# Norm factors put in at eviction, twelve pairs begun ahead, and one PSUM pool, in a hybrid block of two Strassen FFNs and a mixer

## The chip, the core and the metric

The kernel runs on one core of one Trainium2 chip. The metric is the device time of one execution in microseconds (us); lower is better. TensorE (PE in the profile) multiplies matrices into PSUM, a memory of eight banks of 128 x 512 f32; VectorE (DVE), ScalarE (ACT) and GpSimd (POOL) work elementwise; SyncE (SP) issues most DMAs, which move tiles between DRAM and the on-chip SBUF. Each engine runs its own instructions in the order in which the compiler wrote them, and semaphores hold an instruction until its inputs are there.

## The reference: what is computed

The input x has 1024 tokens of width 1024. One layer is applied:

```
h = x + 0.5 * swiglu(rmsnorm(x) , w1_in [1024 x 5632], w1_out [2816 x 1024])
h = h + mixer(rmsnorm(h))          # short convolutions and a gated delta rule
h = h + 0.5 * swiglu(rmsnorm(h), w2_in, w2_out)
out = rmsnorm(h)

swiglu(y) = (silu(y @ w_gate) * (y @ w_up)) @ w_out
rmsnorm(x, w) = x * rsqrt(mean(x * x, axis=-1) + 1e-6) * w
```

All of it is f32. Since rmsnorm multiplies each token by one factor, and each channel by one gain, (factor * gain * x) @ W is the same as factor * ((gain * x) @ W): the factor of a token may be put in before or after a product with weights.

## The kernel before

Tokens lie along the free axis, in two halves of 512; channels lie along the 128 partitions, so x is `h[half][d]`, eight tiles of 128 x 512 per half.

**Products.** A number is held as a rounded part (hi) and the rest (lo), and a product of two such numbers is three matmuls of 128 x 128 by 128 x 512 (`mm3`, lines 196 to 200: whi by hi, whi by lo, wlo by hi). Splitting a tile costs a copy on ScalarE (line 104) and a subtraction on VectorE (line 105). `prod` (line 202) is one block product: four k steps, 12 matmuls into one bank.

**Seven products instead of eight.** Each matrix product is cut in two by two blocks and done by a Strassen-Winograd scheme. For the FFN's input side, a pair is one gate tile and one up tile of 128 columns; `Pair` (line 357) holds its seven products. P1 = B11 by A11 and P2 = B21 by A12 need only the first half of tokens; P1 stays in one bank while it is copied out (`copy_p1`, line 385, ScalarE) and P2 is added onto it in the same bank (`run_p2`). These two are the pair's heads (`head1`, `head2`). The other five products, the body (line 416), use S1 to S4 and A22, which are sums of both halves of tokens (`Blocks.sums`, line 325), and weight sums T1 to T4 made on GpSimd (`pool_tt`) or, for the first two pairs, on VectorE. VectorE evicts them (lines 414 to 452). There are 22 pairs.

**Order.** Work is a list of tasks with three stages (`run_tasks`, line 124): the loads of a task are issued up to nine tasks ahead, its preparation (splits, weight sums) up to four ahead, then it runs. The compiler's scheduler then orders each engine's instructions by priority and estimated readiness, except those under `keep_in_program_order`, which stay behind everything traced earlier on their engine. `later` and `tick` put small steps behind a number of `mm3`s.

**The first stage, in order.** Five pairs' heads run before anything that needs the second half of tokens (`EARLY` = 5). `first_heads` (line 687) loads the eight x tiles, the constants and four B11 tiles; keeps TensorE going with idle matmuls on zeros (`idle`, 34 + 6 + 5 of them); squares and adds the x tiles, sums them over partitions on TensorE (lines 247 to 250), makes the factors (`factor`, line 221, a power on GpSimd), spreads them over partitions (`spread`, line 266, four transposes into a bank), scales x (`norm1`, line 305) and splits it (`split1`). Then come the B11 products of four pairs k step by k step, the fifth pair's P1, and the five P2. The factors of the second half come from row sums of squares (`row_square`, `by_rows`); when they are spread, `x.sums(0)` starts to make S1 and S2. `all_pairs` (line 461) then runs pairs 0 and 1 together, with the heads of two more pairs (`INSIDE` = 2) among their products, then pairs 2 and 3, then one pair at a time; from pair 6 on, the heads of pair i + 1 stand between the products of pair i.

The heads' results P1 and C11 wait in SBUF, in a ring of 21 temporaries, until the body of their pair uses them. The same `all_pairs` serves the mixer's q, k, v projection (six pairs) and the second FFN.

**PSUM.** Each of the three large stages (first FFN with the projection, mixer, second FFN) opens its own PSUM pool (`scoped`, line 660): one tag `ps` with eight banks, or, in the mixer, `mm` and `aux` with four each.

Of the kernel before, what the change touches and what calls it, by code (L numbers as in the profile page):

```python
# [12 lines left out]
P = 128  # L13
# [45 lines left out]
def tile_hybrid(  # L59
# [82 lines left out]
    def psum(tag="ps"):  # L142
        bufs = {"ps": 8, "mm": 4, "aux": 4}[tag]
        return scope["ps"].tile([P, 512], F32, name=f"ps_{tag}", tag=tag, bufs=bufs)
# [64 lines left out]
    class Norm:  # L209
# [25 lines left out]
        def as_they_land(self, idle):  # L235

            idle(34)
            for d in range(KT):
                sq = slot(F32, "sq")
                tc.keep_in_program_order(nc.scalar.activation(out=sq, in_=self.hh[d], func=AF.Square))  # L240
                if d:
                    nc.vector.tensor_tensor(out=self.acc, in0=self.acc, in1=sq, op=ALU.add)
                else:
                    self.acc = sq
# [5 lines left out]
            idle(6)  # L250
# [106 lines left out]
    class Pair:  # L357
# [5 lines left out]
        def __init__(self, x, srcs, first, done):  # L363
            self.x, self.srcs, self.first, self.done = x, srcs, first, done
            self.r, self.t, self.w, self.pinned, self.tt = {}, {}, {}, False, pool_tt
# [14 lines left out]
        def run_p1(self):  # L380
            self.x_ps = psum()
            prod(self.x_ps, self.w.pop("B11"), self.x.b["A11"], True)
            self.copy_p1()

        def copy_p1(self):
            self.p1 = temp4(F32, "p1")
            ins = nc.scalar.copy(out=self.p1[:, 3:HALF + 3], in_=self.x_ps)  # L387
            if self.pinned:
                tc.keep_in_program_order(ins)

        def run_p2(self):
            prod(self.x_ps, self.w.pop("B21"), self.x.b["A12"], False)
            self.done("C11", self.first(self.x_ps))
# [67 lines left out]
    def all_pairs(pairs, x, norm2, between={}, twos=(0, 2)):  # L461


        inside = pairs[EARLY:EARLY + INSIDE]

        def heads_of(some):
            for p in some:
                task(*p.head1())
                task(*p.head2())
# [35 lines left out]
    def gate_pair(x, w_in, j, gs, store):  # L505
        t = {}

        def first(ps):
            c = temp4(F32, "c11")
# [1142 lines left out]
```

## Time and profile before

| | us |
|---|---|
| median of three runs | 1825.29 |
| lowest and highest | 1824.38, 1825.42 |
| the profiled execution's own time | 1825.61 |
| its span, first to last instruction | 1823.9 |
| TensorE busy | 1790.0 (98%) |
| VectorE busy | 1315.3 (72%) |
| ScalarE busy | 742.9 (41%) |
| GpSimd busy | 678.0 (37%) |
| first real product starts (line 197) | 17.80 |

The page gives the busy time of each engine, the span in slices, DMA queues, the chain of work that ended last, and the costliest groups of instructions. Views of the trace give the same by group, by stretch of time, or in order of time; a row in order of time has the start, the duration, the engine, the line, the operation, what it writes and reads, and in brackets how long the engine had been idle and what released it. Matmuls overlap: one of 128 x 512 lasts about 0.39 us but the next starts 0.23 us after it, so the distance of starts is the price of one.

### The profile page before, as it was taken

To read this page: it belongs to the slowest core of one execution; us is meant where nothing else is said; L and a number is where in the kernel's file an instruction comes from. 1 tells how busy PE (TensorE), PEld (TensorE's weight loads), DVE (VectorE), ACT (ScalarE), POOL (GpSimd) and SP (SyncE) were. 2 spreads that over 40 slices of the span, in tenths; PEclk is the share of its full clock that TensorE was granted. 3 is DMA by queue.
4 is the path that set the end of the run, shared out by engine and by line. 5 is a ranking of instruction groups with operands and counts; after the bars stand their busy time and mean duration, and the time that the engine had idled before them with its cause. 6 is when DMAs were issued, how large, how long until landed. Compare 5 with 4: busy or idle time off the path is not lost.

```text
span 1823.9 us, 24890 instructions
## 1 busy us (share of the span) xinstructions
PE 1790.0 (98%) x8509; PEld 1462.3 (80%) x8509; DVE 1315.3 (72%) x2040; ACT 742.9 (41%) x1482; POOL 678.0 (37%) x478
## 2 busy tenths in 40 slices
PE   9999999999999999999899999999999999999997
PEld 6788888888888887777778887788888888888885
DVE  8966666667775888978867576887656666677675
ACT  7423222233534554478242343552222222344443
POOL 0365544445341412325321113006544544435252
PEclk9999999999999999999999999999999999999998
DMA  7243443436984543478664485523433443488642
GB/s 261 70 167 122 136 147 125 135 116 217 326 265 139 168 150 112 137 245 262 221 198 142 133 286 182 177 75 117 160 133 116 144 139 132 163 279 285 215 145 87
DMA packets 194320, 311.41 MB, mean 171 GB/s; under 512 B 28176, under 2 KB 48656, under 8 KB 194192
## 3 DMA queue, kind: packets, MB, share of 16 engines
q1 hardware_dynamic: 191168, 304.51, 50.4%
q10 hardware_dynamic: 3024, 5.30, 0.8%
q8 instruction: 67, 1.10, 0.2%
q14 instruction: 61, 0.50, 0.1%
HBM read 226.87 MB, written 82.86 MB: 170 GB/s over the span
## 4 chain that ended last, share of the span: by engine, by line
PE 85%; DVE 6%; DMA 3%; ACT 3%; issue 2%; POOL 1%; SPq 0%; ACTq 0%; POOLq 0%; DVEq 0%
PE ps_ps L197 24%; PE ps_ps L199 24%; PE ps_ps L198 24%; PE ps_mm L197 3%; PE ps_mm L199 2%; PE ps_mm L198 2%; PE ps_aux L982 1%; DVE cv L884 1%; DMA raw<-w_in 1%; DVE wlo L105 1%; DVE xb L1142 1%; DVE sv L1138 1%; DMA h<-xT 1%; PE ps_aux L1008 0%; DMA qkv_dr<-cv 0%
## 5 line engine op out<-in xcount | busy, mean ns | idle before, releaser
L197 PE MATMUL ps_ps<-hi,whi 128*128 128x512 f32 x1400 | 546.0, 391 | 3.8 <-DVE h L1478 1.5
L198 PE MATMUL ps_ps<-lo,whi 128*128 128x512 f32 x1400 | 545.1, 389 | 0.1
L199 PE MATMUL ps_ps<-hi,wlo 128*128 128x512 f32 x1400 | 544.7, 390 | 0.1
L105 DVE TENSOR_TENSOR wlo<-T,whi 128x512 fp32r<-128x512 f32 x244 | 226.5, 941 | 131.8 <-ACT whi L104 131.1
L105 DVE TENSOR_TENSOR wlo<-raw,whi 128x512 fp32r<-128x512 f32 x280 | 252.9, 914 | 92.1 <-ACT whi L104 87.6
L112 POOL TENSOR_TENSOR T<-raw 128x512 f32<-128x512 f32 x132 | 205.0, 1553 | 302.8 <-DVE wlo L105 108.8
L197 PEld LDWEIGHTS ps_ps<-hi,whi 128*128 128x128 f32 x1400 | 262.7, 188 | 63.7 <-ACT p L387 2.6
L199 PEld LDWEIGHTS ps_ps<-hi,wlo 128*128 128x128 f32 x1400 | 262.8, 188 | 56.1 <-DVE wlo L105 1.7
L198 PEld LDWEIGHTS ps_ps<-lo,whi 128*128 128x128 f32 x1400 | 262.9, 188 | 54.8 <-DVE lo L105 0.8
L197 PE MATMUL ps_ps<-ghi,whi 128*128 128x512 f32 x616 | 241.3, 392 | 0.0
L199 PE MATMUL ps_ps<-ghi,wlo 128*128 128x512 f32 x616 | 240.9, 391 | 0.4 <-DVE wlo L105 0.4
L198 PE MATMUL ps_ps<-glo,whi 128*128 128x512 f32 x616 | 240.6, 391 | 0.0
L104 ACT CAST whi<-raw 128x512 fp32r<-128x512 f32 x280 | 169.0, 617 | 64.0 <-DMA raw<-w_out 21.0
L104 ACT CAST whi<-T 128x512 fp32r<-128x512 f32 x244 | 146.2, 616 | 73.8 <-POOL T L112 34.2
L197 PE MATMUL ps_mm<-hi,whi 128*128 128x512 f32 x384 | 158.5, 413 | 1.2 <-DVE u L452 1.2
L105 DVE TENSOR_TENSOR glo<-raw,ghi 128x512 fp32r<-128x512 f32 x154 | 126.9, 824 | 43.2 <-ACT ghi L104 42.6
L199 PE MATMUL ps_mm<-hi,wlo 128*128 128x512 f32 x384 | 151.6, 395 | 0.0
L198 PE MATMUL ps_mm<-lo,whi 128*128 128x512 f32 x384 | 151.0, 393 | 0.0
L199 PEld LDWEIGHTS ps_ps<-ghi,wlo 128*128 128x128 f32 x616 | 115.8, 188 | 26.5 <-DVE wlo L105 1.0
L198 PEld LDWEIGHTS ps_ps<-glo,whi 128*128 128x128 f32 x616 | 116.1, 188 | 25.6
L197 PEld LDWEIGHTS ps_ps<-ghi,whi 128*128 128x128 f32 x616 | 115.7, 188 | 25.2
L387 ACT COPY p<-ps_ps 128x512 f32<-128x512 f32 x50 | 29.0, 585 | 241.1 <-PE ps_ps L199 241.0
(239 smaller groups left out, 2263.5 us busy)
## 6 DMA issues: line engine op xcount, KB each, us to landing
raw<-w_in SPq DMA_DIRECT2D x264, 256.0 KB, 4.6
raw<-w_out SPq DMA_DIRECT2D x154, 256.0 KB, 4.2
raw<-w_qkv SPq DMA_DIRECT2D x36, 256.0 KB, 3.1
f1S<-S SPq DMA_DIRECT2D x33, 256.0 KB, 5.1
raw<-f1A SPq DMA_DIRECT2D x33, 256.0 KB, 3.6
raw<-f1S SPq DMA_DIRECT2D x33, 256.0 KB, 3.6
f2S<-S SPq DMA_DIRECT2D x33, 256.0 KB, 4.8
raw<-f2A SPq DMA_DIRECT2D x33, 256.0 KB, 4.0
```

What stands on the lines that cost most here:

```text
L104: tc.keep_in_program_order(nc.scalar.copy(out=hi, in_=src))
L105: nc.vector.tensor_tensor(out=lo, in0=src, in1=hi.bitcast(F32), op=ALU.subtract)
L112: tc.keep_in_program_order(nc.gpsimd.tensor_tensor(out=out, in0=in0, in1=in1, op=op))
L197: nc.tensor.matmul(out=ps, lhsT=whi, rhs=xhi, start=start, stop=False, skip_group_check=True)
L198: nc.tensor.matmul(out=ps, lhsT=whi, rhs=xlo, start=False, stop=False, skip_group_check=True)
L199: nc.tensor.matmul(out=ps, lhsT=wlo, rhs=xhi, start=False, stop=stop, skip_group_check=True)
L387: ins = nc.scalar.copy(out=self.p1[:, 3:HALF + 3], in_=self.x_ps)
L884: nc.vector.scalar_tensor_tensor(out=acc, in0=u[:, i:i + HALF], scalar=vcol(wc + i), in1=acc, op0=ALU.mult, op1=ALU.add)
L982: nc.tensor.matmul(out=ps[:, sl], lhsT=lhs[:, sl], rhs=rhs[:, sl], start=start, stop=stop)
L1138: nc.vector.tensor_tensor(out=tv, in0=lrow[:, lo:hi].unsqueeze(2).broadcast_to([nb, n, j + 1]), in1=xrow[:, 0:j + 1].unsqueeze(1).broadcas ...
L1142: nc.vector.tensor_tensor(out=xv, in0=xv, in1=tv, op=ALU.subtract)
```

## The change

- In the first FFN, x is multiplied by its gain alone and split as it lands (`split_raw`); the factor of a first-half token is multiplied in when P1 is copied out and before Silu of C11, both on VectorE, from a copy of the spread factors in SBUF (`rb0`, which shares its place with the later `rb2`). x is still scaled in place afterwards, for S1 to S4. Loads are issued in the order x tile 0, four B11, x tiles 1 to 7, constants; rows for the second half's sums and the second half itself follow at given tasks.
- The idle matmuls are 12 instead of 45. The sums of squares, the factors and their spread come behind the four B11 products; the fifth pair's P1 stands between sums and spread.
- Nine pairs' heads run ahead (before five) and three among pairs 0 and 1 (before two). Of these twelve, pairs 5 to 11 write P1 and C11 to DRAM (`spill`, `put`) and read them back while the pair before runs (`fetch`).
- In all three uses of `all_pairs`, the P1 of an inside pair stands ahead of the last k step of the S1 and S2 products, or between two other products, instead of right before its P2.
- One PSUM pool serves the whole kernel, with tags `mm` and `aux` of four banks; a request for `ps` takes them in turn.

```diff
+    pp = ctx.enter_context(tc.tile_pool(name="pp", bufs=1, space=PS))
+    turn = [0]
+
+    def psum(name="ps"):
+        tag = name
+        if name == "ps":
+            tag = ("mm", "aux")[turn[0] % 2]
+            turn[0] += 1
+        return pp.tile([P, 512], F32, name=f"ps_{name}", tag=tag, bufs=4)
...
+        def spill(self, p1, c11):
+            self.dr = p1, c11
+
+        def put(self, i, tile_):
+            if self.dr is not None:
+                nc.sync.dma_start(out=self.dr[i], in_=tile_[:, 3:HALF + 3])
+
+        def fetch(self):
+            self.p1 = temp4(F32, "p1")
+            nc.sync.dma_start(out=self.p1[:, 3:HALF + 3], in_=self.dr[0])
+            c = temp4(F32, "c11")
+            nc.sync.dma_start(out=c[:, 3:HALF + 3], in_=self.dr[1])
+            self.done("C11", c)
+
         def copy_p1(self):
             self.p1 = temp4(F32, "p1")
-            ins = nc.scalar.copy(out=self.p1[:, 3:HALF + 3], in_=self.x_ps)
-            if self.pinned:
-                tc.keep_in_program_order(ins)
+            if self.rb is None:
+                nc.scalar.copy(out=self.p1[:, 3:HALF + 3], in_=self.x_ps)
+            else:
+                nc.vector.tensor_tensor(out=self.p1[:, 3:HALF + 3], in0=self.x_ps, in1=self.rb, op=ALU.mult)
+            self.put(0, self.p1)
...
+        now, soon = inside[:max(1, len(inside) - 1)], inside[max(1, len(inside) - 1):]
...
                 for k in range(KH):
+                    if k == KH - 1:
+                        task(*now[0].head1())
                     task(lambda k=k: [p.both(k) for p in pairs[:2]])
-                heads_of(inside[:1])
+                for p in now[1:]:
+                    task(*p.head1())
+                for p in now:
+                    task(*p.head2())
...
-                    for t in two:
-                        task(*t)
-                if a == 0 and n == 2:
-                    heads_of(inside[1:])
+                    task(*two[0])
+                    for p in soon if a == 0 and n == 2 else ():
+                        task(*p.head1())
+                    task(*two[1])
+                    for p in soon if a == 0 and n == 2 else ():
+                        task(*p.head2())
...
         for i in range(twos[-1] + 2, len(pairs)):
             body = list(pairs[i].body())
-            if EARLY + INSIDE <= i + 1 < len(pairs):
+            if i + 1 < len(pairs) and pairs[i + 1].dr is not None:
+                body[2:2] = [(None, pairs[i + 1].fetch)]
+            if n_early + n_inside <= i + 1 < len(pairs):
                 body[2:2] = [pairs[i + 1].head1()]
                 body[4:4] = [pairs[i + 1].head2()]
...
         def first(ps):
             c = temp4(F32, "c11")
+            if rb is not None:
+                nc.vector.tensor_tensor(out=c[:, 3:HALF + 3], in0=ps, in1=rb, op=ALU.mult)
+                ps = c[:, 3:HALF + 3]
             nc.scalar.activation(out=c[:, 3:HALF + 3], in_=ps, func=AF.Silu)
...
+        def split_raw(d):
+            src, gain = h[0][d], x.gain(d)
+            hi, lo = slot(F32R, "hi"), slot(F32R, "lo")
+            tc.keep_in_program_order(nc.scalar.activation(out=hi, in_=src, func=AF.Copy, scale=gain))
+            nc.vector.scalar_tensor_tensor(out=lo, in0=src, scalar=gain, in1=hi.bitcast(F32),
+                                           op0=ALU.mult, op1=ALU.subtract)
+            x.b["A11" if d < KH else "A12"][d % KH] = hi, lo
...
             for k in range(KH):
-                first(k)
...
+                task(lambda k=k: run(k))
+            task(norms[0].all_landed)
+            f, g, l = early[4].head1()
+            task(lambda: f(False), g, l)
+            task(scaled)
+            task(*early[5].head1())
+            for i in range(4):
+                second(i)
+            for i in range(4, len(early)):
+                if i == 5:
+                    task(norms[1].spread)
+                if i + 2 < len(early):
+                    task(*early[i + 2].head1())
+                second(i)
-        g_dr = ffn_in(x, norms, w1_in, "f1", first_heads)
+        g_dr = ffn_in(x, norms, w1_in, "f1", first_heads, rb0, 5, 9, 3)
```

`second(i)` is the P2 of early pair i with steps of the second half beside it: row squares, `by_rows`, `norm1`, `begin2`, and the loads of rows and of the second half. `scaled` spreads the first half's factors, copies them to `rb0` and scales the P1 of the first five pairs out of PSUM.

More of the change, by code (lines that the diff above doesn't have):

```diff
@@ L233, in reduce, with landed, all_landed @@
             self.factor(cp[:, 0:4])
[L235 to L244, printed above, removed]
+        def landed(self, d):
+            sq = slot(F32, "sq")
+            tc.keep_in_program_order(nc.scalar.activation(out=sq, in_=self.hh[d], func=AF.Square))
+            if d:
+                nc.vector.tensor_tensor(out=self.acc, in0=self.acc, in1=sq, op=ALU.add)
+            else:
+                self.acc = sq
+        def all_landed(self):
             cp = psum(self.bank)
@@ L459, in body, with all_pairs @@
             yield run_p3, lambda: self.ready("B22")
[L461 to L469, printed above, removed]
+    def all_pairs(pairs, x, norm2, between={}, twos=(0, 2), n_early=EARLY, n_inside=INSIDE):
+        inside = pairs[n_early:n_early + n_inside]
+        now, soon = inside[:max(1, len(inside) - 1)], inside[max(1, len(inside) - 1):]
         for p in pairs[:2]:
@@ L523, in done, with ffn_in @@
                 store(j, hf)
-        return Pair(x, (w_in[j, 0], w_in[j, 1]), first, done)
+        pair = Pair(x, (w_in[j, 0], w_in[j, 1]), first, done)
+        pair.rb = rb
+        return pair
     G_BLOCKS = ("A11", "A12", "A22", "S1", "nS2", "S3", "S4")
-    def ffn_in(x, norms, w_in, name, start=None):
+    def ffn_in(x, norms, w_in, name, start=None, rb=None, kept=EARLY + INSIDE, early=EARLY, inside=INSIDE):
         gs = {}
@@ L554, in store @@
                     later(8 + 5 * i, lambda args=args: make(*args))
-        pairs = [gate_pair(x, w_in, j, gs, store) for j in range(NJ)]
-        if start is None:
-            early_heads(pairs[:EARLY])
-        else:
-            start(pairs)
-        all_pairs(pairs, x, norms[1])
+        pairs = [gate_pair(x, w_in, j, gs, store, rb) for j in range(NJ)]
+        for i in range(kept, early + inside):
+            pairs[i].spill(dram.tile([P, HALF], F32, name=f"{name}p{i}"), dram.tile([P, HALF], F32, name=f"{name}c{i}"))
+        (start or early_heads)(pairs[:early])
+        all_pairs(pairs, x, norms[1], n_early=early, n_inside=inside)
         return g_dr
@@ L703, in first_heads, with get_rows @@
             idle_ps = psum()
[L705 to L712 removed]
+            for _ in range(12):
+                tc.keep_in_program_order(
+                    nc.tensor.matmul(out=idle_ps, lhsT=zero[:, 0:P], rhs=zero, start=True, stop=True))
             for p in four:
                 p.x_ps = psum()
[L715 to L720 removed]
+            for d in range(KT):
+                split_raw(d)
+                if d == 0:
+                    for p in four:
+                        p.ready("B11")
+                if d == KH - 1:
+                    for e in range(KT):
+                        norms[0].landed(e)
+                elif d < KH:
+                    pass
+            rows2 = []
+            def get_rows(*bs):
+                for b in bs:
+                    for i in range(2):
+                        rows2.append(slot(F32, "xtok"))
+                        tc.keep_in_program_order(nc.sync.dma_start(out=rows2[-1], in_=xtok[b][:, i, :]))
             def run(k):
@@ L725, in run @@
                     mm3(p.x_ps, w[0][:, ks], w[1][:, ks], *x.b["A11"][k], k == 0, k == KH - 1)
-                if k == KH - 1:
-                    for p in four:
-                        p.w.pop("B11")
-                        p.copy_p1()
-                    norms[1].spread()
-            for k in range(KH):
-                first(k)
-            def then():
-                for d in range(KH, KT):
-                    first(d)
-                norms[1].by_rows()
-                for k in range(KH):
-                    x.begin2(k)
@@ L742, in first_heads, with scaled @@
-            task(lambda: run(0), then, lambda: get_x(1, 0, 4, 1, 5, 2, 6, 3, 7))
-            for k in range(1, KH):
-                task(lambda k=k: run(k))
-            task(*early[4].head1())
-            for p in early:
-                task(*p.head2())
-        g_dr = ffn_in(x, norms, w1_in, "f1", first_heads)
+            def scaled():
+                norms[0].spread()
+                nc.scalar.copy(out=rb0, in_=norms[0].rb)
+                for p in four:
+                    p.w.pop("B11")
+                    p.copy_p1()
+                early[4].copy_p1()
```

67 lines of the change are left out of this document (33 added, 34 removed).

## The prediction

> **What bounds the kernel now.** I read the head of the page first, then the busy time by stage, then the first 31 us of TensorE in order of time, then TensorE's waits one by one.
>
> ```profile
> span 1823.9 us, 24890 instructions
> PE 1790.0 (98%) x8509; PEld 1462.3 (80%) x8509; DVE 1315.3 (72%) x2040; ACT 742.9 (41%) x1482; POOL 678.0 (37%) x478
> PE 85%; DVE 6%; DMA 3%; ACT 3%; issue 2%; POOL 1%; SPq 0%; ACTq 0%; POOLq 0%; DVEq 0%
> ```
>
> TensorE is busy 98% of the span and carries 85% of the chain that ended last. So what counts is when its first real product starts, what stands between its products, and nothing else until another engine falls behind it.
>
> ```profile
> core 0: us, PE busy (x) PEld busy (x) DVE busy (x) ACT busy (x) POOL busy (x), PEclk, DMA share, GB/s
> 0.00:17.80 17.80, 13.80 (x58) 6.06 (x58) 9.23 (x18) 9.62 (x17) 3.09 (x9) 1.00 0.92 329
> 29.20:46.60 17.40, 17.31 (x79) 14.07 (x77) 17.40 (x30) 14.17 (x27) 0.00 (x0) 1.00 0.37 121
> 46.60:60.00 13.40, 13.40 (x60) 10.87 (x59) 13.40 (x23) 5.75 (x10) 0.00 (x0) 1.00 0.13 42
> 111.00:139.00 28.00, 28.00 (x123) 22.47 (x121) 17.16 (x24) 4.94 (x9) 13.48 (x10) 1.00 0.49 168
> 177.00:405.00 228.00, 228.00 (x1007) 188.79 (x1006) 146.30 (x168) 65.70 (x120) 111.09 (x72) 1.00 0.39 132
> ```
>
> Two prices come from here. In steady state 1007 matmuls take 228 us, 0.2264 us each, so a product of 12 matmuls is 2.72 us. And from 29.2 to 60 us VectorE is never idle: 53 instructions in 30.8 us, 0.58 us each (0.60 below). It is the second bound of the first stage and must be watched.
>
> ```profile
> 1.32 9.70 PE L708 MATMUL ps_ps<-zero 128*128 128x512 bf16 x34 [1.32 <-DVE zero L702]
> 5.13 0.15 PEld L708 LDWEIGHTS <-zero 128*128 128x128 bf16 x1 [0.28 <-issue]
> 5.56 0.15 PEld L708 LDWEIGHTS <-zero 128*128 128x128 bf16 x1 [0.28 <-issue]
> 5.89 4.63 PEld L708 LDWEIGHTS <-zero 128*128 128x128 bf16 x22 [0.18 <-issue]
> 12.87 1.05 PE L248 MATMUL ps_ps<-one,sq 128*128 128x1 f32 x8 [1.85 <-DVE sq L242]
> 13.79 1.46 PE L708 MATMUL ps_ps<-zero 128*128 128x512 bf16 x6
> 14.21 1.40 POOL L225 TENSOR_TENSOR rs<-ms,cs 128x4 f32<-128x4 f32 x1 [11.92 <-DVE ms L223]
> 15.66 0.65 PE L271 MATMUL ps_ps<-cs,rs 128*128 128x128 f32 x4 [0.42 <-POOL rs L225]
> 16.14 1.24 PE L708 MATMUL ps_ps<-zero 128*128 128x512 bf16 x5
> 17.80 1.20 PE L197 MATMUL ps_ps<-hi,whi 128*128 128x512 f32 x4 [0.41 <-ACT hi L104]
> 29.22 0.60 PE L271 MATMUL ps_ps<-cs,rs 128*128 128x128 f32 x4
> ```
>
> The busy TensorE of the first 17.8 us is idle matmuls (line 708) and the norm's own (lines 248, 271). The first real product starts at 17.80; the four B11 products of four pairs end where the second norm's spread starts, 29.22.
>
> **Part 1, the earlier start.** The change multiplies x by its gain alone, so the products no longer wait for the norm, and loads x tile 0, the four B11, then x tiles 1 to 7. When do they land?
>
> ```profile
> 3.95 1.13 ACT L240 ACTIVATE sq<-h 128x512 f32<-128x512 f32 x2
> 6.06 3.96 ACT L240 ACTIVATE sq<-h 128x512 f32<-128x512 f32 x6 [0.98 <-DMA h<-xT]
> 10.87 2.55 ACT L104 CAST whi<-raw 128x512 fp32r<-128x512 f32 x4 [0.85 <-DMA raw<-w_in]
> ```
>
> All are 256 KB tiles in one queue, so I go by position. The first had landed by 3.95, the third landed at 6.06, the tenth (x's eight, the constants, then a B11) at 10.87: about 0.68 us apart. So now x0 is there at 3.9, the B11 at 4.5, 6.1, 6.8 and 7.4, x1 at 8.1, x2 at 8.8, x3 at 9.4, x7 at 12.2. Cast and subtraction (0.62 and 0.73, rows of part 3) put the last B11's low part at 8.8 and x1's at 9.4. The first step's 12 matmuls run as weights arrive and end near 9.1; the second loses 0.3 us to x1's low part; then 36 × 0.227 = 8.2, so the four products end at about 17.5 instead of 29.2: **+11.7**. Bounds: 12.0 with no wait at all, 10.2 if each of the three later x tiles costs 0.5 us more.
>
> TensorE's clock: the idle matmuls start 0.43 us apart until 5.56, after which 22 come in 4.63 us (0.21). Twelve of them then end at about 6.1 with the fast rate just reached. The Trainium skill, "TensorE: Matmul & The Clock Gate", Part 1 on the HAM clock gate, says that the clock is released by about 3.4 us of sustained activity in a free-running window; the trace agrees with 4.2 us here. By that rule the gaps while weights land could cost one more window at half rate, 1.7 us, and the sum would be 9.8 instead of 11.5; by the row (full rate at 13.79 after the pause that ended at 12.87) it costs nothing, which I take.
>
> **Part 2, the norm moves onto TensorE's path.** The column sums (12.87 to 13.79, 0.9) and the spread (15.66 to 16.14, 0.5) ran ahead of the products and now stand among them: **−1.4**. Must TensorE wait? Squares and adds run behind x3's split on ScalarE and VectorE: 8 × 0.57 (two took 1.13) from 10.1, the last add 0.7 later, done at 15.4, before 17.5. After the sums (18.4) come one scale and POOL's 1.40: 20.2; the fifth pair's product covers until 21.1. Without that cover the wait would be 1.8. Bound: 0 to −1.8 more; I take 0.
>
> **Part 3, VectorE's added work.** In the first stage all 22 pairs' P1 copies leave ScalarE for VectorE, and C11 gets a multiplication ahead of Silu.
>
> ```profile
> L387 ACT COPY p<-ps_ps 128x512 f32<-128x512 f32 x22 | 12.6, 585 | 113.4 <-PE ps_ps L199 113.4
> L441 DVE TENSOR_TENSOR c<-ps_ps,p 128x512 f32<-128x512 f32 x22 | 15.0, 681 | 9.9 <-PE ps_ps L199 9.9
> L307 DVE SCALAR_TENSOR_TENSOR h<-h,vs,ps_ps 128x512 f32<-128x512 f32 x8 | 5.7, 742 | 1.0 <-PE ps_ps L271 1.0
> L105 DVE TENSOR_TENSOR lo<-h,hi 128x512 fp32r<-128x512 f32 x24 | 17.2, 725 | 0.0
> L104 ACT CAST whi<-T 128x512 fp32r<-128x512 f32 x88 | 52.2, 616 | 20.0 <-POOL T L112 14.4 <-PE ps_ps L198 3.9 <-DVE T L117 1.7
> ```
>
> That is 44 × 0.68 = 30 us on VectorE, which in 177 to 405 is 64% busy: 22 pairs over some 420 us make it 71%; there TensorE covers it. The crowded place is the start. TensorE now reaches the S1 products at 17.5 + 1.9 (sums, both spreads) + 14 × 2.72 (five heads more to give 9 P1 and 9 P2, less the four done) = 57.5. VectorE must by then have done, from the first scaled copy at 22.6 on (spread until 21.6, a copy of the factor, its start): 9 copies, 9 multiplications, 8 norms, 4 begins of half two, 9 low parts of weights, the first S1/S2 block (4), and T1, T2 of two pairs (8): 51 × 0.60 = 31, done at 53.6. Slack 4 us. S3 needs some 42 more (25 us, at 79), when TensorE, after 4 × 2.72 of S1/S2 and 4 × 2.72 of two inside pairs, is at 79.3. So it just holds, if the order is right. Bounds 0 and −6; I take **−1**.
>
> **Part 4, the order of heads, and fuller pairs.**
>
> ```profile
> 72.08 0.50 PE L197 MATMUL ps_ps<-hi,whi 128*128 128x512 f32 x1 [0.68 <-ACT p L387]
> 1227.31 0.50 PE L197 MATMUL ps_ps<-hi,whi 128*128 128x512 f32 x1 [0.68 <-ACT p L387]
> 138.74 0.39 PE L199 MATMUL ps_ps<-hi,wlo 128*128 128x512 f32 x1
> 139.21 0.50 PE L197 MATMUL ps_ps<-hi,whi 128*128 128x512 f32 x1
> ```
>
> Twice a P2 waits for the copy of its own P1. Another product now stands between in both FFNs: 0.84 each in starts of matmuls (0.68 idle plus the refill): **+1.7**, bounds 0 and 1.7. Against it: pairs 4 to 10 run without a head inside (now two pairs do, 111 to 139, with 123 matmuls where 28 us hold 123.7; the worst gap is the 0.24 us extra at 138.74). Five more such pairs at 0.3: **−1.5**, bounds 0 and −5, since they also take 0.5 MB each from DRAM: 28 transfers, at 0.68 us 19 us of a queue that is 0.39 to 0.49 busy.
>
> **Part 5, one PSUM pool.**
>
> ```profile
> 781.38 0.68 DVE L452 TENSOR_TENSOR u<-ps_ps,u 128x512 f32<-128x512 f32 x1
> 782.21 0.47 PE L197 MATMUL ps_mm<-hi,whi 128*128 128x512 f32 x1 [1.18 <-DVE u L452]
> 1172.36 0.68 DVE L1478 TENSOR_TENSOR h<-ps_mm,h 128x512 f32<-128x512 f32 x1
> 1173.19 0.47 PE L197 MATMUL ps_ps<-hi,whi 128*128 128x512 f32 x1 [1.52 <-DVE h L1478]
> ```
>
> At both changes of pool the first product waits for the last reader of the old pool, whose data it doesn't use. A rotating pool has a free bank. At 1173 the products that follow are independent: I take 1.3 of 1.5. At 782 the mixer is held by its VectorE and DMA chain soon after, so the gain may be waited away: 0.7 of 1.2. **+2.0**, bounds 0 and 2.7.
>
> **Sum.** 11.7 − 1.4 − 1 + 1.7 − 1.5 + 2.0 = 11.5 us. The profiled execution took 1825.61 in all (span 1823.9 and 1.7 around it), 0.3 above the median 1825.29. So 1825.6 − 11.5 = 1814.1, or **1814** beside the median.
>
> **Rivals.** (a) VectorE orders the first 80 us: late copies or S blocks make TensorE wait. For it: no idle VectorE from 29 to 60 now. Against: no wait of TensorE there now either, and the added heads bring 27 us of matmuls for 5 × 4 × 0.60 = 12 us of VectorE. With 0.15 us more for each of the 51, 7.6 less the slack of 4: 1818; with both places late 1821. (b) The dense pairs 4 to 10 become bound by transfers, POOL and VectorE: 1 us for each of seven instead of 0.3, 5 lost: 1819. (c) Slower: the eviction on VectorE stands behind a blocked low part. Place: the heads inside pairs 10 to 20, eleven of them, where only one product (2.72) lies between P1 and P2. If the copy is late by w, TensorE loses 11 w; it decides from 11.5 / 11 = 1.05 us, and at 1.5 the time is 1830. Against it: line 441's eviction now stands as close to its next product, and TensorE has no idle time from 177 to 405. (d) The change doesn't do what it says: TensorE starts early but S1/S2/S3, built from both halves of x, come at their old time behind more VectorE work; 1824 to 1826. Against it: the 4 us of slack above. (e) Nothing is lost anywhere: 12.0 − 1.4 + 1.7 + 2.7 = 15, 1810, and a mixer schedule that falls well could add 1 or 2.
>
> **How the numbers follow.** The forecast has 0.55, (a) 0.17, (b) 0.08, (c) 0.08, (d) 0.06, (e) 0.06. A measurement of this kernel tells about 0.2% (3.7 us) from no change, so faster holds all but (c) and (d): 0.86; same 0.06; slower 0.08. The range goes from just under (e), 1809, to (a) with both places late, 1821, and leaves out (c), (d) and tails.
>
> **What would show it.** Right: the first matmul of line 197 at about 6, the four B11 products done at 17 to 18, VectorE without long idle before 57, no wait at line 387's successor, no 1.5 us gap where the pool changed, 177 to 405 still full. Wrong: a wait of TensorE on VectorE (a P1 copy, h, or lo) of over 1 us between 20 and 85, gaps once per pair between pairs 4 and 20, or a mixer that takes longer than its 390 us (782 to 1173).

## The result, and the profile after

The changed kernel takes 1841.2 us in the median of six runs (1837.75 to 1846.82); the kernel before, on the same chip, 1824.99 (1823.24 to 1825.42, six runs). The ratio is 1.0088, with a 95% interval from 1.0078 to 1.0099. The change makes the kernel 16 us slower; the forecast was 11.5 us faster, and the range ended at 1821. Further down, one execution of 2543 us and one of 4608 us, far above all others of their kernels, are left out of the medians and spreads.

The profiled execution took 1837.75 (the shortest of the six), 12.1 more than the profiled one of before. The figures by stage and by wait below are of such single profiled executions. The head of its page:

```profile
span 1836.0 us, 24965 instructions
PE 1786.8 (97%) x8476; PEld 1457.5 (79%) x8476; DVE 1351.2 (74%) x2084; ACT 729.6 (40%) x1457; POOL 677.2 (37%) x478
```

VectorE has 36 us more to do. TensorE is still the engine that counts, but its busy share fell although 33 idle matmuls are gone. The start, in TensorE's order of time:

```profile
1.31 4.58 PE L742 MATMUL ps_ps<-zero 128*128 128x512 bf16 x12 [1.31 <-DVE zero L738]
5.63 0.50 PE L203 MATMUL ps_ps<-hi,whi 128*128 128x512 f32 x1
9.40 0.50 PE L204 MATMUL ps_ps<-lo,whi 128*128 128x512 f32 x1 [0.21 <-DVE lo L726]
```

The first real product starts at 5.63 instead of 17.80, and the second k step loses 0.2 us to x1's low part. So the early start is there. Counting the real matmuls from the start of the program, the 48th starts at 17.24 instead of 28.99: 11.75 us ahead. Then the lead goes: 10.45 us at the 73rd (25.04 against 35.49), 7.2 at the 121st (39.1 against 46.4), 4.7 at the 481st (125.0 against 129.7), −6.2 at the 921st (236.2 against 230.0), −8.2 when the first FFN's output side begins (443.18 against 435.02).

Busy times by stretch of time, after (us; PE, PEld, DVE, ACT, POOL with their instructions, then granted clock, DMA share, GB/s):

```profile
158.00:237.00 79.00, 72.36 (x311) 57.30 (x310) 56.65 (x61) 16.52 (x30) 46.17 (x30) 1.00 0.45 151
790.00:950.00 160.00, 143.36 (x753) 116.43 (x753) 124.05 (x284) 88.86 (x222) 50.83 (x40) 0.98 0.72 231
```

The same stretches of before; the mixer starts there at 782:

```profile
158.00:237.00 79.00, 79.00 (x350) 65.44 (x349) 50.04 (x58) 24.28 (x45) 39.31 (x26) 1.00 0.38 127
782.00:942.00 160.00, 149.39 (x812) 123.23 (x813) 126.96 (x297) 97.25 (x239) 56.92 (x44) 0.98 0.74 237
```

From 158 to 237 TensorE was full and is now idle for 6.6 us. The mixer's first 160 us hold 6 us less of it. Elsewhere the two kernels run alike: output side of the first FFN and projection 347.2 and 346.9 us, second FFN 416.5 and 415.5, its output side 223.2 and 223.3; the mixer takes 396.5 instead of 391.0. That is 8.2 + 5.5 − 1.2, or 12.5 us at TensorE's last matmul; what follows it is 0.3 us shorter, which leaves 12.1 of span.

What TensorE waited for in the whole run, after (total us, times, longest):

```profile
PE ps_ps L205 <- DVE wlo L105: 5.3, 6, 1.8
PE ps_ps L203 <- ACT whi L104: 4.9, 4, 1.3
PE ps_aux L1045 <- DVE gd L1174: 4.6, 2, 3.0
PE ps_ps L203 <- DVE u L457: 4.2, 3, 1.5
```

The `ps_ps` rows are nearly all the first FFN's, the `ps_aux` rows the mixer's.

**The seven pairs without heads.** These are pairs 4 to 10. From 155 to 235 there is one wait in each of pairs 5 to 10, of 1.55 to 1.91 us from start to start where 0.23 is normal (9.1 us in sum). Pair 4 has none; a shorter one, 0.79, at 127.5 belongs to pairs 2 and 3 before it. One of the six, VectorE in order of time:

```profile
168.62 0.68 DVE L477 TENSOR_TENSOR u<-ps_ps,u 128x512 f32<-128x512 f32 x1
169.22 1.18 DVE L105 TENSOR_TENSOR wlo<-raw,whi 128x512 fp32r<-128x512 f32 x1
170.33 1.78 DVE L555 TENSOR_TENSOR u<-u,c 128x512 f32<-128x512 f32 x1
172.03 0.68 DVE L457 TENSOR_TENSOR u<-ps_ps,p 128x512 f32<-128x512 f32 x1
```

and TensorE and GpSimd at the same place (GpSimd was on another weight sum until 171.5):

```profile
171.12 0.39 PE L205 MATMUL ps_ps<-hi,wlo 128*128 128x512 f32 x1
171.52 1.72 POOL L112 TENSOR_TENSOR nS<-u,S 128x512 f32<-128x512 f32 x1
172.85 0.47 PE L203 MATMUL ps_ps<-hi,whi 128*128 128x512 f32 x1 [1.34 <-ACT whi L104]
```

The matmul at 172.85 opens P7, which is added onto P6's bank, so it must wait until VectorE has read P6 out (line 457, done at 172.71). Its weights had been cast at 165.6: the cast that the row names is only the last semaphore that came, for another product. GpSimd itself was not late either: it had made the weight sums of this pair by 156.2. The reading of P6 stands third in VectorE's order, behind a low part of weights and the gate product (line 555). With 0.60 us from start to start, as everywhere on a free VectorE, it would have ended 1.6 us earlier, and P7 would have followed at 171.35. But the two instructions ahead, which read two tiles of SBUF, take 1.18 and 1.78 us while GpSimd is at work; those that read PSUM keep their 0.68. In before, one such pair had the same order and no wait:

```profile
129.80 0.68 DVE L105 TENSOR_TENSOR wlo<-T,whi 128x512 fp32r<-128x512 f32 x1
130.40 0.68 DVE L521 TENSOR_TENSOR u<-u,c 128x512 f32<-128x512 f32 x1
131.00 0.68 DVE L432 TENSOR_TENSOR u<-ps_ps,p 128x512 f32<-128x512 f32 x1
132.43 0.39 PE L197 MATMUL ps_ps<-hi,whi 128*128 128x512 f32 x1
```

GpSimd did nothing there; P6 was out at 131.68, 0.75 us before P7. In the pairs of before that have heads inside, the instructions were stretched too:

```profile
182.74 1.77 DVE L521 TENSOR_TENSOR u<-u,c 128x512 f32<-128x512 f32 x1
184.44 1.79 DVE L105 TENSOR_TENSOR wlo<-raw,whi 128x512 fp32r<-128x512 f32 x1
186.15 0.68 DVE L432 TENSOR_TENSOR u<-ps_ps,p 128x512 f32<-128x512 f32 x1
187.40 0.39 PE L197 MATMUL ps_ps<-hi,whi 128*128 128x512 f32 x1
```

But there one of the next pair's heads, its P1, stands between P5 and P7, so that the products between P6 and P7 last 5.4 us instead of 2.7. (The other head, P2, stands behind P7.) VectorE reads P6 out until 186.83, and P7 starts at 187.40 without a wait; 2.7 us earlier, at 184.7, it would have had to wait for 2.1 us (an estimate from these rows). That the missing head is what uncovers the eviction is read from the two orders; no run puts a head back into these pairs.

All VectorE tensor_tensor instructions on 128 x 512 f32 of the changed kernel's trace show the same: 630 with two SBUF tiles and no GpSimd sum beside them took at most 0.70 us; 133 with such a sum beside them for over 95% of their time took 1.77 in the median; 393 that read PSUM took at most 0.70, sum or not. The Trainium skill, "GPSIMD Engine Reference", Specifications, says that GpSimd's SBUF interfaces are shared with VectorE, with contention for VectorE instructions that have two SBUF inputs. The trace agrees in which instructions suffer, with the 1.77 against 0.70 us above.

**The first 100 us.** VectorE and ScalarE where TensorE stands still for 0.93 and 1.71 us:

```profile
30.55 0.69 DVE L409 TENSOR_TENSOR p<-ps_ps,rb 128x512 f32<-128x512 f32 x1
31.15 1.28 DVE L542 TENSOR_TENSOR c<-ps_ps,rb 128x512 f32<-128x512 f32 x2
...
34.01 1.41 DVE L311 SCALAR_TENSOR_TENSOR h<-h,vs,rb 128x512 f32<-128x512 f32 x2
35.33 0.75 DVE L322 SCALAR_TENSOR_TENSOR h<-h,vs 128x512 f32<-128x512 f32 x1
35.99 0.69 DVE L105 TENSOR_TENSOR wlo<-raw,whi 128x512 fp32r<-128x512 f32 x1
...
31.87 0.63 ACT L544 ACTIVATE c<-c 128x512 f32<-128x512 f32 x1 [2.32 <-DVE c L542]
33.64 0.60 ACT L104 CAST whi<-raw 128x512 fp32r<-128x512 f32 x1
...
36.73 0.50 PE L205 MATMUL ps_ps<-hi,wlo 128*128 128x512 f32 x1 [1.71 <-DVE wlo L105]
```

ScalarE stands in front of Silu for 2.32 us, because the new multiplication by the factor (line 542) comes behind copies and norms on VectorE; the cast of the next weights is queued behind Silu and two scalings, and TensorE waits for it first. Their low part comes 2.35 us after the cast, because VectorE makes three tiles of norm (34.01 to 36.0) before it; that is the longer wait. Two more waits of 1.2 and 2.0 us, at 80.2 and 96.8, are again VectorE's: u2 (the reading of P6), and low parts.

### The profile page after: what moved, and what is told of

Same layout as the page of the kernel before. It is cut to its first block, busy times and chain, and to the rows that moved or that the text cites. A ratio compares the mean times of both kernels' runs of the same rounds, so it can differ in the third digit from the quotient of the medians.

```text
span 1836.0 us, 24965 instructions
## 1 busy us (share of the span) xinstructions
PE 1786.8 (97%) x8476; PEld 1457.5 (79%) x8476; DVE 1351.2 (74%) x2084; ACT 729.6 (40%) x1457; POOL 677.2 (37%) x478
## 4 chain that ended last, share of the span: by engine, by line
PE 49%; DVE 2%; DMA 1%; issue 1%; ACT 1%; POOL 1%; SPq 0%; ACTq 0%; POOLq 0%; DVEq 0%
PE ps_ps L203 12%; PE ps_ps L205 11%; PE ps_ps L204 11%; PE ps_mm L203 3%; PE ps_mm L204 3%; PE ps_mm L205 3%; PE ps_aux L1045 1%; PE ps_aux L1071 1%; DVE xb L1205 0%; PE ps_aux L1051 0%; PE ps_aux L1300 0%; DVE sv L1201 0%; PE ps_aux L1299 0%; DVE cv L947 0%; PE ps_mm L1338 0%
## 5 line engine op out<-in xcount | busy, mean ns | idle before, releaser
L203 PE MATMUL ps_ps<-hi,whi 128*128 128x512 f32 x1400 | 547.1, 392 | 11.5 <-ACT whi L104 4.9
L105 DVE TENSOR_TENSOR wlo<-raw,whi 128x512 fp32r<-128x512 f32 x280 | 246.7, 892 | 71.3 <-ACT whi L104 70.3
L105 DVE TENSOR_TENSOR wlo<-T,whi 128x512 fp32r<-128x512 f32 x244 | 229.2, 953 | 91.7 <-ACT whi L104 88.2
L104 ACT CAST ghi<-raw 128x512 fp32r<-128x512 f32 x154 | 95.0, 617 | 69.1 <-DMA raw<-f2A 19.5
```

What stands on the lines that cost most here:

```text
L104: tc.keep_in_program_order(nc.scalar.copy(out=hi, in_=src))
L105: nc.vector.tensor_tensor(out=lo, in0=src, in1=hi.bitcast(F32), op=ALU.subtract)
L203: nc.tensor.matmul(out=ps, lhsT=whi, rhs=xhi, start=start, stop=False, skip_group_check=True)
```

## The experiments

In all of them "before" was run on the same chip, with medians from 1825.13 to 1825.62. Where kernels are compared that ran on different chips, that "before" is the common measure.

**Theory and rivals.** Theory: the time is lost where VectorE's results come late in the first FFN (order and GpSimd's stretching), and, apart from that, in the mixer through the single pool. Rivals: the transfers of kept P1 and C11; GpSimd itself late with weight sums; too many heads ahead.

### One PSUM pool alone

Before, with the pool of the change.

```diff
-    def psum(tag="ps"):
-        bufs = {"ps": 8, "mm": 4, "aux": 4}[tag]
-        return scope["ps"].tile([P, 512], F32, name=f"ps_{tag}", tag=tag, bufs=bufs)
+    pp = ctx.enter_context(tc.tile_pool(name="pp", bufs=1, space=PS))
...
-        scope["ps"] = stack.enter_context(tc.tile_pool(name=name + "ps", bufs=1, space=PS))
```

> The kernel before with only the single PSUM pool of the change. The prediction had the pool at 2.0 us faster (1823). Theory A (the pool is harmless and the mixer's 5.5 us lost in the changed kernel come from a new schedule around it): 1821 to 1826, with the waits for the last reader at 782 and 1173 gone. Theory B (two rings of four hold the mixer or the FFNs up): slower by 4 to 6 us, 1829 to 1831, with longer waits of TensorE between 782 and 1173.

1831.96 (1829.28 to 1835.07, five runs), ratio 1.0035 [1.0022, 1.0048]: 6.4 us slower. The wait at the first change of pool went, as forecast (that stage 1.2 us shorter), and the mixer became 7.4 us longer, 398.4: TensorE stands idle there for 18.1 us instead of 14.3, and is busy for 3.7 us more, since the granted clock is 0.5 for 13.7 us of the mixer instead of 6.8. (In the changed kernel it is 6.8 as before; there 4.9 of the 5.5 us are idle time.) TensorE's waits from 780 to 960, before:

```profile
PE ps_aux L982 <- ACT gd L1063: 6.2, 3, 4.8
PE ps_aux L988 <- DMA gd<-qkv_dr: 1.5, 2, 1.2
```

and with the one pool:

```profile
PE ps_aux L987 <- DVE gd L1116: 4.6, 2, 3.0
PE ps_aux L1013 <- DMA xc<-diag_x: 2.5, 1, 2.5
PE ps_aux L993 <- DMA gd<-qkv_dr: 2.4, 2, 1.9
```

The waits are others, and longer in sum. Compared tile by tile, about one in nine of the mixer's matmuls (250 of 2292) stands elsewhere in the compiled order when the kernel has one pool. The four profiled kernels with one pool all have this one order and take 396.5 to 401.6 us for the mixer; the ten with three pools all have the other, and take 390.1 to 391.9 in eight, 394.2 in one and 398.0 in one that was at half clock for 17 us of it. That the order is the cause is likely, but no run separates it from the banks themselves.

### The change with the three old pools

After, with the three lines removed above put back.

> The changed kernel with the three old pools in place of the single one. Theory A: within 3 us of the changed kernel (1841), the dense pairs 4 to 10 as slow as there (1.5 us a pair). Theory B (the pool costs the mixer 5.5 us): 1834 to 1836. If the two rings of four are what makes the dense pairs slow, those gaps go and it is 1830 or less.

1836.55 (1835.9 to 1843.17, four runs), ratio 1.0059 [1.0042, 1.0076]. The rest of the change costs 11.0 us by itself; with the pool's 6.4 that is 17.4, against the 16.2 of the whole. The six waits of the pairs without heads are the same, 1.68 to 1.73 us. So the two losses are separate. The profiled execution is the slowest of the four (1843.17); the 398.0 above is its mixer.

### The gate product later

After; C12 · C11 and the store of its result are put behind ten more small steps, so that they needn't stand ahead of P6's eviction.

```diff
+                if rb is not None and hf == 0:
+                    later(10, gated)
+                else:
+                    gated()
```

> The changed kernel with the first half's gate product (C12 times C11) and its store put ten mm3 later, so that VectorE reaches the eviction of P6 (u2), which P7 waits for, earlier. Theory C (VectorE's order, stretched by GpSimd, makes P7 late by 1.5 us in each dense pair): six gaps of 1.5 to 1.9 us between 150 and 240 shrink to under 0.6, 6 to 9 us faster than the changed kernel, 1832 to 1835. Theory D (transfers or GpSimd's sums bind these pairs): the same gaps elsewhere in the pair, within 2 us of 1841.

1837.85 (1835.3 to 1838.95, four runs), 1.0065 [1.005, 1.008]. The six waits fell from 1.7 to 0.61 (start to start, so 0.4 idle), as the theory of the order wants. But VectorE's compiled order changed elsewhere too: there is one new wait of 2.75 us at 143 and one of 1.68 at 248. The first FFN is 3 us shorter than after, and no more; the time lies between the spans of the two theories (1832 to 1835, and within 2 us of 1841).

### Without GpSimd's sums of gated blocks

After; S1, nS2, S3 and S4 of the gated blocks of pairs 0 to 11 are left out (a gated block is stored in their place).

```diff
                 def make(n, p, q, op):
+                    if rb is not None and j <= 11:
+                        put(n, k, p)
+                        return
```

> The changed kernel without GpSimd's sums of gated blocks for pairs 0 to 11 of the first FFN (S1, nS2, S3, S4 are stored as their first operand instead; the output is another, the transfers are the same). Theory C with contention: VectorE's 1.2 to 1.8 us instructions in the dense pairs fall to 0.7, the gaps there shrink to under 0.5, 6 to 10 us faster, 1831 to 1835. Rival (VectorE's order alone, GpSimd without part in it, or transfers): gaps stay above 1 us, 1838 to 1842.

1836.64 (two runs), 1.0061 [1.0041, 1.0081]. VectorE by group, 150 to 240, with the sums:

```profile
L105 DVE TENSOR_TENSOR wlo<-T,whi 128x512 fp32r<-128x512 f32 x24 | 25.6, 1107 | 0.0
L555 DVE TENSOR_TENSOR u<-u,c 128x512 f32<-128x512 f32 x6 | 10.6, 1773 | 0.0
L466 DVE TENSOR_TENSOR c<-ps_ps,p 128x512 f32<-128x512 f32 x6 | 4.2, 692 | 7.1 <-PE ps_ps L205 7.1
```

and without:

```profile
L105 DVE TENSOR_TENSOR wlo<-T,whi 128x512 fp32r<-128x512 f32 x26 | 17.2, 700 | 0.0
L555 DVE TENSOR_TENSOR u<-u,c 128x512 f32<-128x512 f32 x6 | 7.4, 1228 | 0.0
L472 DVE TENSOR_TENSOR p<-ps_ps,p 128x512 f32<-128x512 f32 x7 | 4.8, 692 | 14.4 <-PE ps_ps L205 14.4
```

The same instructions, and nearly the same order (411 of VectorE's 416 up to the end of the pairs; TensorE's and ScalarE's are equal): the low parts fall from 1107 to 700 ns and the gate products from 1773 to 1228; what reads PSUM keeps 692. Waits remain in every other pair only, of about 0.6, and the first FFN ends 5.7 us earlier than after. The stretching by GpSimd is shown. The time is above the 1831 to 1835 expected, because the mixer of this execution took 401.6 us instead of 396.5, at half clock for 17 us instead of 6.8.

### Each kept tile read back twice

After with three pools; every kept P1 and C11 is fetched a second time into an unused tile: 14 more transfers of 256 KB.

```diff
+            for d in self.dr:
+                again = temp4(F32, "again")
+                nc.sync.dma_start(out=again[:, 3:HALF + 3], in_=d)
```

> The changed kernel with the three old pools (1836.5) in which each spilled P1 and C11 is read back twice, 14 more transfers of 256 KB among pairs 4 to 10. Theory C (VectorE's order and GpSimd bind the dense pairs, transfers don't): within 2 us of it, 1835 to 1839. Theory D (transfers or SyncE's queue bind these pairs): 0.65 us for each transfer, 7 to 10 us slower, 1844 or more.

1833.87 (1833.12 to 1839.47, four runs), 1.0051 [1.0032, 1.0069]: not slower than the same kernel without them (1836.55, on another chip). The transfers don't bind.

The trace shows one thing more. TensorE, VectorE and ScalarE have the same order as with three pools alone, but only three of the six waits are left (at 173, 202 and 232, 1.7 from start to start). In each of the three pairs whose wait went, a weight landed later, and GpSimd began its sum as the gate product ended, or after it, instead of beside it. The first of them:

```profile
157.85 0.68 DVE L552 TENSOR_TENSOR u<-u,c 128x512 f32<-128x512 f32 x1
158.39 1.29 POOL L112 TENSOR_TENSOR T<-raw,T 128x512 f32<-128x512 f32 x1 [1.01 <-DMA raw<-w_in]
```

With three pools alone, where TensorE waits at 158.90 for 1.71 from start to start:

```profile
157.58 1.73 POOL L112 TENSOR_TENSOR T<-raw,T 128x512 f32<-128x512 f32 x1
158.09 1.77 DVE L549 TENSOR_TENSOR u<-u,c 128x512 f32<-128x512 f32 x1
```

So with an unchanged order the wait comes and goes with GpSimd.

### Gate product and first Silu later

After with three pools; the gate product as above, and Silu of C11 with its store behind six small steps, against the wait at 33 to 37.

```diff
+            if self.rb is None:
+                rest()
...
+                later(6, rest)
```

> The changed kernel with the three old pools, the gate product ten mm3 later and the Silu of C11 (with its store) six mm3 later. Theory C and E (E: in the first 40 us ScalarE stands still before Silu, which waits for VectorE's late multiplication, and the next low parts come late): the 3 us of waits between 33 and 37 go as well as 3 of the dense pairs; 1830 to 1833 against 1836.5. If E is wrong, the waits at 33 to 37 stay and it is 1833 to 1835.

1830.3 (1827.4 to 1833.52, ten runs), 1.0028 [1.0018, 1.0037]. The six waits are 0.61 to 0.63 again, and one of 3.1 us appears at 142. At 33 to 37 TensorE still waits, once for 2.34 from start to start instead of twice: Silu still stands ahead of the cast in ScalarE's compiled order. So the time lies in the span of 1830 to 1833 although the wait that was to go for it did not.

### Seven pairs ahead and two inside

After with three pools, five of the pairs in SBUF, four in DRAM.

```diff
-        g_dr = ffn_in(x, norms, w1_in, "f1", first_heads, rb0, 5, 9, 3)
+        g_dr = ffn_in(x, norms, w1_in, "f1", first_heads, rb0, 5, 7, 2)
```

> The changed kernel with the three old pools, and seven pairs begun ahead and two inside instead of nine and three, so that four pairs in place of seven run without a head inside. Theory C (each dense pair costs 1.5 us): 4.5 us less, if VectorE has S1 and S2 ready 5.4 us of matmuls earlier; 1831 to 1833. Rival (VectorE needs the nine pairs' matmuls as cover): a wait of 4 to 8 us before the S1 and S2 products, 1836 to 1840.

1837.2 (1834.32 to 1839.8, four runs), 1.0062 [1.0046, 1.0078]. Fewer pairs without heads, but TensorE stands still from 64.9 to 72.4. TensorE and VectorE there:

```profile
72.42 0.77 PE L197 MATMUL ps_ps<-hi,whi 128*128 128x512 f32 x1 [7.11 <-ACT whi L104]
...
71.59 0.68 DVE L403 TENSOR_TENSOR p<-ps_ps,rb 128x512 f32<-128x512 f32 x1
```

The product that starts at 72.42 is the P2 of an inside pair, added onto its P1's bank; P1 had been ready since 62.5, and its copy (line 403) comes at 71.59, at the end of the S work in VectorE's order. The time is in the span of the rival (1836 to 1840). So nine pairs ahead are not too many: without them the S blocks are still being made when the inside pairs run, and the copy is queued behind them.

### The order of heads alone

Before, with the new place of the inside pairs' P1 in all three uses, and nothing else.

```diff
+                    if k == KH - 1:
+                        task(*now[0].head1())
...
+                    task(*two[0])
+                    for p in soon if a == 0 and n == 2 else ():
+                        task(*p.head1())
```

> The kernel before with only the new order of the inside pairs' heads. The prediction had it at 1.7 us faster, 1823.9, with the two waits of a P2 for its own P1's copy (70.9 and 1226) gone. Rival: the time stays within 1 us, because what was waited for there is waited for later.

1824.48 (1822.94 to 1827.78, ten runs), 0.9995 [0.9986, 1.0004]. Both waits for the copy of the own P1 (72.08 and 1227.31 of before) are gone; the spans of the profiled executions differ by 1.9 us (1822.0 against 1823.9), the medians by 1.1. The interval includes no change, so the gain is not shown by time.

### The gate product pinned behind P6's eviction

After with three pools; the gate product of a half is issued behind the eviction of the next pair's P6 instead of so many steps later. Silu of C11 is kept behind the casts that were prepared before it.

```diff
+            ins = nc.scalar.activation(out=c[:, 3:HALF + 3], in_=ps, func=AF.Silu)
+            if rb is not None:
+                tc.keep_in_program_order(ins)
...
+                    if rb is not None and hf == 0 and u2_ins[0] is not None:
+                        with tc.issue_after(u2_ins[0].ins):
+                            nc.vector.tensor_tensor(out=g, in0=g, in1=t["C11"], op=ALU.mult)
```

> The changed kernel with the three old pools (1836.5); the gate product of the first half is issued behind the next pair's u2 eviction, and Silu of C11 behind the casts that were prepared before it. If order is what makes P7 late and the low parts of the fourth P2 late: the gaps of 1.7 us in pairs 4 to 10 under 0.4 (9 us), the 3 us at 33 to 37 under 1, 1824 to 1828. If VectorE has too much work rather than the wrong order: the gaps come back at another product, 1831 or more.

1829.4 (1827.22 to 1830.84, nine runs), 1.0019 [1.0009, 1.0028]. Six waits became three, of 1.72 from start to start, and no new one came between 125 and 240. What TensorE waited for from 150 to 240:

```profile
PE ps_ps L197 <- DVE u L453: 4.0, 3, 1.3
```

They lie in every other pair, at 170.8, 200.0 and 229.2, where GpSimd makes the gated blocks' sums and a stretched low part still stands ahead of the eviction. At 34.5 the wait for the cast is gone, but the one for its low part is 2.42 from start to start, since VectorE makes norms before it; under 1 was expected. The time is between the two spans expected (1824 to 1828, and 1831 or more). This is the best version of the change found, 7 us better than with three pools alone, and still 4.3 slower than before.

### Weight sums on VectorE

After with three pools; T1 to T4 of pairs 4 to 10 on VectorE instead of GpSimd.

> The changed kernel with the three old pools, and the weight sums T1 to T4 of pairs 4 to 10 on VectorE instead of GpSimd: more work for VectorE (28 instructions), none for GpSimd there but the gated blocks' sums. Theory C (VectorE is late since GpSimd's instructions beside it stretch its own from 0.68 to 1.2 to 1.8 us): VectorE's instructions there back at 0.7, gaps smaller, 1829 to 1833. Rival (VectorE simply has too much to do in these pairs): 28 x 0.68 = 19 us more on it, gaps of 2 us and more, 1838 to 1845.

1838.64 (1837.49 to 1840.4, four runs), 1.0071 [1.0054, 1.0088]. VectorE by group, 150 to 240:

```profile
L105 DVE TENSOR_TENSOR wlo<-T,whi 128x512 fp32r<-128x512 f32 x24 | 21.8, 951 | 0.0
```

The low parts are less stretched (951 against 1060 with three pools), but the sums themselves now stand in VectorE's order, and there are more waits, not fewer: eight of 0.6 to 2.2 us between 125 and 240. The time is the rival's (1838 to 1845).

### Both

The two edits before this one together.

> Both edits together. If order and stretching are two parts of one lateness, little more than the better of the two alone, 1823 to 1828; if each removes waits of its own, 1820 to 1824, below the kernel before.

1836.48 (1834.66 to 1837.84, three runs), 1.0058 [1.0041, 1.0075], far above both spans expected (1820 to 1828). The pinning gains little once VectorE has the sums.

### Pinned, and without GpSimd's sums

The pinned kernel, without S1 to S4 of the gated blocks of pairs 0 to 11, as above.

> The kernel with the gate product pinned behind u2, and without GpSimd's sums S1, nS2, S3, S4 of the gated blocks of pairs 0 to 11 (a gated block is stored in their place, so the DMAs stay; the output is another). In the pinned kernel three waits of 1.72 us stay, at 170.77, 200.01 and 229.24, one in every other dense pair, those in which GpSimd makes the sums. Theory A (GpSimd's sums stretch VectorE's instructions that still stand ahead of u2): the three waits shrink to 0.6 or less each, the first FFN ends 3 to 5 us earlier than 438.3, at 433 to 435, and the time is 1825 to 1827. Theory B (what remains is VectorE's order alone): the waits stay within 0.3 of 1.72 and the end of the first FFN within 1 us of 438.3, time 1829 to 1830. If the clock falls to half after a wait, the time is 2 to 6 us above either, and the end of the first FFN still tells them apart.

1825.15 (1823.46 to 1827.12, ten runs), 0.9996 [0.9987, 1.0006]. From 150 to 240:

```profile
PE ps_ps L197 <- DVE u L453: 1.4, 3, 0.9
...
L105 DVE TENSOR_TENSOR wlo<-T,whi 128x512 fp32r<-128x512 f32 x24 | 19.1, 817 | 0.0
```

The three waits are 0.61, 0.67 and 1.28 from start to start instead of 1.72: GpSimd's stretching made more than half of what the order had left. The time is in the span that this theory expected; the end of the first FFN, 437.3, is not (433 to 435 was expected, and 438.3 in the pinned kernel), since this execution lost 1.5 us more before 112 us than the pinned one: it was at half clock twice there (from 37.0 and from 101.9, 3.4 us each) instead of once. And with all that work left out the kernel only equals the one before.

## Why the prediction was wrong

**Part 1, the earlier start (+11.7): right**, 11.75 measured. The rival reading of the clock, one more window at half rate at the start, did not come: but for the wait at 9.4 the starts are 0.23 us apart from 6.7 on.

**Part 2, the norm on TensorE's path (−1.4, no wait): right in the net, with luck.** From the 48th to the 73rd matmul the lead fell by 1.3. Sums and spread took 1.2, near the forecast. A wait of 0.6 us for a low part at 19.1 was not forecast, but before has its second spread (0.35) and a wait of 0.25 in the same stretch; the change has its second spread later, at 44.6.

**Part 3, VectorE's added work (−1, bounds 0 and −6): mis-sized, at the end of its bounds.** The lead fell from 10.45 to 4.7 by 125 us; the four waits make 6.1, and the gain of the head order and the late spread are in the difference too. The sum "51 × 0.60" counted how much VectorE has to do by 57.5 us, and that held; what failed is "if the order is right". The waits come from single instructions out of place: the multiplication before Silu, with a cast queued behind it on ScalarE (1.1 us), the norms ahead of that cast's low part (1.9), u2 (1.2) and other low parts (2.0). This is rival (a) in engine and size; (a) had named late copies and S blocks, which are not what TensorE waited for.

**Part 4, the head order (+1.7): right in sign**, both waits gone; the run that makes this edit alone is 1.1 us faster, which is not clear of no change.

**Part 4, the fuller pairs: the step that failed.** "Five more such pairs at 0.3: −1.5, bounds 0 and −5" was priced from two pairs of before in which GpSimd happened to stand still while VectorE made the gate product and the eviction (from 116.4 to 118.2 and from 127.5 to 136.7, waiting for loads). Measured: 1.3 to 1.7 us in each of six pairs, 9.1 in sum, and the lead went from 4.7 to −6.2 by 236 us, 10.9 us. It is beyond its own bound. Rival (b), 1 us for each of seven, had the place right, and GpSimd and VectorE among its causes, at two thirds of the size; it named transfers first, and the run that doubles the reads rules those out. What was missed is what a head did in every pair of before from 6 on: P1 of the next pair stood between P6 and P7 and covered VectorE's eviction. The rows were there: in before, from 150 to 240, the low parts take

```profile
L105 DVE TENSOR_TENSOR wlo<-T,whi 128x512 fp32r<-128x512 f32 x20 | 20.3, 1032 | 15.5 <-ACT whi L104 15.5
```

on average 1032 ns, not 600. With P5 alone, 2.72 us, as cover, one stretched low part, one stretched gate product and the eviction behind them don't fit. In which pairs TensorE waits follows GpSimd: the waits shrink or go when its sums are left out or come later.

**Part 5, one pool (+2.0, bounds 0 and 2.7): wrong in sign.** The two waits vanished as described; the mixer then took 5.5 us longer in the profiled execution, and the edit alone costs 6.4. The step that failed is that the pool changes nothing but these two waits. The text's last line on what would show it wrong, a mixer longer than its 390 us, is what came. That the pool reorders the program of another stage was not among the steps; "the gain may be waited away" was the closest, and it bounded the loss at nothing.

**Rivals.** (a) and (b) both came, together with a loss in the pool that none held. Rival (c), a copy of P1 that comes late on VectorE, came small at its place: the heads stand inside pairs 11 to 20 (ten, not eleven), and P2 waits for that copy by 0.25 us in every other one, five in all, where 1.05 us in each would have decided. Its mechanism is what the run with seven pairs ahead shows, for 7 us. (d), no gain from the early start, fell with Part 1. Each rival was worked out as if the others stayed at nothing, and the range ended where one alone would end it.

**The sum with measured terms**, for the profiled execution: 11.75 − 1.3 (norm) − 5.75 (VectorE to 125 us, the head order's gain inside it) − 10.9 (to 236 us, 9.1 of it the six pairs) − 2.0 (from there on) = −8.2; then −5.5 in the mixer and +1.2 elsewhere: −12.5 at TensorE's last matmul. The median of the six is 3.5 us worse than that execution; their mean clock goes from 0.995 in it down to 0.990.

**Open:** whether the mixer's order or its banks cost the 6 us. Even the pinned kernel without the sums is 2.3 us behind at the end of the first FFN (437.3 against 435.0) after having been 11.6 ahead. Its trace says where most of this goes: 7.1 us in four waits up to 101 us (low parts, and u2), about 3 at half clock, 1.9 in the three pairs; no run removes all four. No version tried is faster than before.

## What to carry to other kernels

Before a product is moved out of a stage to start it earlier, look at what it covers where it stands: here a head hid an eviction that the next product needs, and most of the 11.75 us of earlier start was paid back at 1.5 us a pair. Price an elementwise instruction from rows in which the same neighbours are at work (with two SBUF tiles 0.68 us alone, 1.2 to 1.8 beside GpSimd), and count the queue ahead of the one that TensorE waits for rather than the engine's total. A shared allocation, as a PSUM pool, is an edit to every stage that uses it: measure it alone.

## What the hardware showed unexpectedly

**After a wait of little over 2 us TensorE's clock can be halved.** The pinned kernel, by stretch of time:

```profile
96.00:100.00 4.00, 2.11 (x10) 1.45 (x9) 4.00 (x7) 1.14 (x2) 0.97 (x2) 0.99 0.11 41
100.00:103.40 3.40, 3.40 (x10) 2.65 (x9) 3.40 (x4) 0.00 (x0) 2.81 (x2) 0.50 0.44 131
```

After a wait that lasted from 97.24 to 99.52 from start to start (1.9 us idle) the granted clock is 0.50 for 3.4 us, with starts 0.427 us apart; that costs 1.7 us on top of the wait. The changed kernel's profiled execution had a wait of 2.21 us at the same place and kept its clock; the changed kernel without GpSimd's sums of gated blocks, whose matmuls have the same order there, had one of 2.21 too, and its clock was 0.50 from 100.3 on for 3.4 us. In the mixer the half clock lasts 6.8 us in both profiled executions (from 886 before, from 940 after). So waits of the same length cost more in some executions than in others. That fits the wider spread of the changed kernel, though no run shows that it is the cause: 9 us over six runs after, 2.2 over six of before, 4.3 over nineteen of before on another chip. The Trainium skill, "TensorE: Matmul & The Clock Gate", Part 1, gives a free-running window of about 3.4 us and an idle window as what lowers the clock; the 3.4 us agree, but 1.9 us of idleness was enough here.

**GpSimd slows only some of VectorE's instructions, and those by much.** Beside a GpSimd sum a VectorE tensor_tensor with two SBUF tiles of 128 x 512 f32 took up to 1.81 us in the changed kernel instead of 0.68, and the ones that read PSUM stayed at 0.69 or less. The averages over a stage hide this.
